# One-hot matrices and gated rows of a table building laid out token by token instead of eight tokens interleaved

## The chip, the cores and the metric

The kernel runs on one core of one Trainium2 chip. The metric is the device time of one launch in microseconds, the median of three runs. The engines work in parallel, each through its own list of instructions in order: TensorE (PE; its weight loads are PEld) multiplies matrices, VectorE (DVE) and ScalarE (ACT) work element by element, GpSimd (POOL) does some element work and issues the row gathers, SyncE (SP) issues the plain transfers.

## The reference

Two layers of a transformer over 512 latent tokens and 256 context tokens, 1024 wide. Each layer mixes tokens (three kinds of heads, one output projection) and then retrieves experts. The change touches the second part alone: each token has 8 heads, each head selects 16 of 16384 experts by a product key (two lists of 128 sub-keys, so an expert is a pair of numbers i and j below 128) and weighs them by a softmax.

```python
def peer(h, wq, subkeys, u, v):
    """sum_heads sum_topk g_e * gelu(u_e . h) * v_e."""
    ...
    s_top, i_top = lax.top_k(s, PEER_TOPK)
    cand = (s_top[:, :, 0, :, None] + s_top[:, :, 1, None, :]).reshape(...)
    ...
    best, pos = lax.top_k(cand, PEER_TOPK)
    expert = jnp.take_along_axis(cand_idx, pos, axis=-1)
    gate = jax.nn.softmax(best, axis=-1)
    ...
        a = jax.nn.gelu(jnp.einsum('cd,chkd->chk', hc, u[ec]), approximate=False)
        w = (gc * a).astype(v.dtype)
        return jnp.einsum('chk,chkd->cd', w, v[ec])
```

## The kernel before

Tokens stand in tiles of 128; the first layer has six (four latent, two context), the second four. After mixing and output projection, `peer` runs in stages.

A u-pass (`upass`, two halves of 64 columns of experts) multiplies the whole first expert matrix with three of the tiles and keeps the gelu of it, two tiles' worth in a table in SBUF, the third spilled to DRAM. These three tiles are called dense. The remaining tiles (three in the first layer, one in the second) are handled by gathers: `gather` fetches 128 expert rows a token, one DMA_INDIRECT for each of the 128 choices (L920, on GpSimd), and VectorE multiplies them with the token (L926). Gathers are generators, moved on at fixed rates between the other work.

Then a v-pass (`vpass`) for each pair of tiles multiplies a table over all experts (the summed gate of each expert, times the gelu) with the second expert matrix: 128 steps of 12 matmuls of 512 columns (L1060) in two halves. Each step loads a 128x1024 block, copies it to f16 on ScalarE (L1043) and takes the rest on GpSimd (L1047) or VectorE (L1045).

The table is built by `Scatter`. For a token the 128 choices stand along partitions; one-hot rows of i (128 wide) and of j (64 wide, the half of the table in work), the latter multiplied with the gate, are multiplied by TensorE and give the token's 128x64 table. The gate stands as two f16 parts whose sum is the f32 value, so a token takes two matmuls on the same one-hot weights (L1172 on the high part, L1173 on the low part). Eight tokens make one step: `oi` (L1167, 1024 elements a partition), `oj` (L1168, 512), `oh` and `ol` (L1169, L1170, 512 each) on VectorE, 16 matmuls into one PSUM tile `pw`, and then the evacuation into the table: VectorE multiplies it in (L1178, for the first pair), or ScalarE copies it (L1180, L1182) with VectorE taking the rest (L1183) for gathered tiles. All buffers but `oj` (one) are double. In `oi`, `oj`, `oh` and `ol` the eight tokens are the innermost dimension: element (k, x) belongs to choice number k and token x, and a matmul takes every eighth element.

`prep` (L1131 to L1145) brings a tile's choices and gates from tokens along partitions to choices along partitions through TensorE: `sT` holds i, j, the gate's high and its low part.

Where the steps stand is set by the generators in `vpass` and `upass`: after every second large step of a v-pass one step of the coming half's table is put into all engines' lists (`next(ahead, None)`), and in the second half of a u-pass from the twelfth step on by a rate (`SC0`). A half of a table is 32 steps: two tiles of 16. Ten such halves are built, five pairs of tiles in two halves each. The vector tables `st16` and `io16` are used by `pick`, which turns the top-16 lists into expert numbers.

Of the kernel before, what the change touches and what calls it, by code (L numbers as in the profile page):

```python
# [9 lines left out]
F16 = mybir.dt.float16  # L10
# [3 lines left out]
AF = mybir.ActivationFunctionType  # L14
OP = mybir.AluOpType
# [13 lines left out]
TB = 8  # L29
# [20 lines left out]
class Hybrid:  # L50
# [20 lines left out]
    # ---------------------------------------------------------------- constants  # L71
    def consts(self):
# [11 lines left out]
        self.iox = c.tile([128, 128, TB], F16, name="iox")  # L84
        nc.vector.tensor_copy(self.iox, io[:, :, None].to_broadcast([128, 128, TB]))
        self.io16 = c.tile([128, 16, 8], F16, name="io16")
        nc.vector.tensor_copy(self.io16, io[:, :16, None].to_broadcast([128, 16, 8]))
        self.st16 = c.tile([128, 2, 16, 8], F16, name="st16")
        prev = 0
        for a, s in enumerate((0, 16, 24, 29, 33, 36, 38, 40, 42, 43, 44, 45, 46, 47, 48, 49)):  # L90
            nc.vector.memset(self.st16[:, 0, a], float(s))
            nc.vector.memset(self.st16[:, 1, a], float(s - prev))
            prev = s
# [20 lines left out]
    def tick(self, gens, rate):  # L114
        """Moves the generators on by rate on the average."""
        self.due = getattr(self, "due", {})
        k = id(gens)
        self.due[k] = self.due.get(k, 0.0) + rate
        n = int(self.due[k])
        self.due[k] -= n  # L120
        self.step(gens, n)
# [57 lines left out]
    # ---------------------------------------------------------------- modulation  # L179
# [33 lines left out]
    def vectors(self, l, last, pool, ps):  # L213
        """The factors that vary along a row, written out as rows."""
        nc = self.nc
# [19 lines left out]
    # ---------------------------------------------------------------- layer  # L235
# [37 lines left out]
    # ---------------------------------------------------------------- mixers  # L273
# [203 lines left out]
    # ---------------------------------------------------------------- attention  # L477
# [171 lines left out]
    def strips(self, l, h, pool):  # L649
        """Decay by distance: forwards over positive, backwards over negative distances, both at zero."""  # L650
# [28 lines left out]
    # ---------------------------------------------------------------- output projection, second norm  # L679
# [80 lines left out]
    # ---------------------------------------------------------------- product-key routing  # L760
# [72 lines left out]

    def pick(self, l, t, sv, si, pool):
# [65 lines left out]
    # ---------------------------------------------------------------- gathered first expert matrix  # L900
# [35 lines left out]
    # ---------------------------------------------------------------- experts  # L936
# [4 lines left out]
    def peer(self, es, l, last, h2s):  # L941
# [10 lines left out]
        with ExitStack() as e:  # L952
            rp = self.pool(rk, "rk", 2)
            rt = self.pool(e, "rt", 2, side="right")
# [135 lines left out]
class Scatter:  # L1090
    """Sums the gates of a pair of tiles into a table over all experts; over given values the sums are multiplied in."""
# [7 lines left out]
    def col(self, half, jj, n=1):  # L1099
        """The table's columns jj.. of a half."""  # L1100
# [7 lines left out]
    def at(self, half, jj):  # L1108
        """The stationary operands of expert column jj: a pair of parts for each token tile."""
# [21 lines left out]
    def prep(self, t):  # L1131
# [10 lines left out]
        sT = o.sp.tile([128, 4, 128], F16, name="sT", bufs=2)  # L1142
        nc.scalar.activation(sT[:, 0:3], p[:, :384].rearrange("p (a b) -> p a b", b=128), AF.Copy)
        nc.vector.tensor_tensor(sT[:, 3], p[:, 256:384], sT[:, 2], op=OP.subtract)
        self.sT[t] = sT  # L1145

    def step(self, half):
# [6 lines left out]
        for s in sorted(range(2), key=lambda s: not self.dense[s]):  # L1154
# [3 lines left out]
            sT = self.sT[t]  # L1158
            for tb in range(0, 128, 8):
                pp = o.pw.tile([128, 8, 64], F32, name="pw")  # L1160
                for t0 in range(tb, tb + 8, TB):
                    oi = o.sp.tile([128, 128, TB], F16, name="oi")
                    oj = o.sp.tile([128, 64, TB], F16, name="oj", bufs=1)
# [92 lines left out]
```

## Time and profile before

| | us |
|---|---|
| median of three runs | 5032.78 (5029.45 to 5037.81) |
| the profiled execution, first to last instruction | 5040.9 |
| TensorE matmul busy | 4516.0 (90%) |
| TensorE weight load busy | 2857.2 (57%) |
| VectorE busy | 3624.2 (72%) |
| ScalarE busy | 2209.1 (44%) |
| GpSimd busy | 2221.1 (44%) |

A busy time is the union of an engine's recorded instructions. Matmuls overlap in the pipeline and their ends are modelled, so the pace of a burst is read from the starts of its instructions in the timeline. A row of the costliest groups gives line, engine, operation, tiles, shape and count, then busy us, mean ns, and the idle time before them with what ended it. A busy time of VectorE holds the time in which an instruction has been started and stands still.

### The profile page before, as it was taken

The numbers are of one execution on the slowest core, as the hardware profiler recorded it, in microseconds if no ns is written. First come the engines' busy times: TensorE is split into PE (matmuls) and PEld (weight loads), VectorE is DVE, ScalarE is ACT, GpSimd is POOL, SyncE is SP. The second block draws the span as 40 slices with busy tenths as digits, with TensorE's granted clock in tenths as the row PEclk, the third lists the DMA queues.
The fourth block names the chain that finished last, engine by engine and source line by source line (L and its number), as shares of the span: only waits on it lengthen the run. The fifth ranks groups of instructions, "written<-read, shape, count | busy, mean of one in ns | idle before, by whom it ended". The sixth has DMA issues, their size and how long they took to land. (4 is left out here: it accounts for less than half of the span.)

```text
span 5040.9 us, 79837 instructions
## 1 busy us (share of the span) xinstructions
PE 4516.0 (90%) x30416; PEld 2857.2 (57%) x30416; DVE 3624.2 (72%) x7163; ACT 2209.1 (44%) x3694; POOL 2221.1 (44%) x1493
## 2 busy tenths in 40 slices
PE   4987888978999988998899999788878999998998
PEld 3664566745665554554555467455545766655553
DVE  7777549897889999988798245745775777667543
ACT  5556344343433343433334466644444443343443
POOL 4224133457566665555233422422456544443333
PEclk9996999989999998999899999799999999998999
DMA  5421446668777767877578632144657764445555
GB/s 180 150 65 35 156 134 208 194 196 282 249 255 251 247 245 256 290 256 277 188 235 270 202 122 66 39 145 134 208 183 251 249 222 149 143 151 166 168 188 176
DMA packets 379873, 955.15 MB, mean 189 GB/s; under 512 B 43632, under 2 KB 158800, under 8 KB 379488
## 3 DMA queue, kind: packets, MB, share of 16 engines
q1 hardware_dynamic: 296000, 675.74, 41.6%
q0 software_dynamic: 73888, 268.53, 15.0%
q10 hardware_dynamic: 9600, 5.77, 0.4%
q8 instruction: 238, 3.90, 0.3%
q14 instruction: 147, 1.20, 0.1%
HBM read 920.49 MB, written 29.41 MB: 188 GB/s over the span
## 5 line engine op out<-in xcount | busy, mean ns | idle before, releaser
L1047 POOL TENSOR_TENSOR hl<-s,hl 128x1024 f16<-128x1024 f32 x384 | 861.8, 2244 | 1077.0 <-ACT hl L1043 1075.1
L1060 PE MATMUL acc<-hl,gst 128*128 128x512 f16 x3456 | 835.4, 391 | 17.6 <-DVE gst L149 9.0
L926 DVE SCALAR_TENSOR_TENSOR r<-r,hp 128x1024 f32<-128x1024 f32 x512 | 619.4, 1213 | 284.0 <-DMA r<-peer_u,ix 283.1
L1043 ACT ACTIVATE hl<-s 128x1024 f16<-128x1024 f32 x480 | 505.2, 1057 | 697.7 <-PE acc L1060 313.5
L1060 PEld LDWEIGHTS <-gst 128*128 128x128 f16 x4608 | 463.9, 101 | 565.6 <-issue 58.5
L920 POOL DMA_INDIRECT r<-peer_u,ix x512 | 547.2, 1069 | 391.5 <-DVE r L926 193.1
L1172 PE MATMUL pw<-oh,oi 128*128 128x64 f16 x2560 | 640.1, 300 | 72.0 <-DVE oh L1169 70.7
L1173 PE MATMUL pw<-ol,oi 128*128 128x64 f16 x2560 | 639.9, 301 | 13.7 <-DVE ol L1170 13.5
L1060 PE MATMUL acc<-hl,P 128*128 128x512 f16 x2304 | 558.5, 389 | 5.2 <-POOL hl L1047 3.1
L1060 PEld LDWEIGHTS <-P 128*128 128x128 f16 x3072 | 307.8, 100 | 354.1 <-issue 27.7
L1172 PEld LDWEIGHTS <-oi 128*128 128x128 f16 x2560 | 372.5, 146 | 133.9 <-DVE oh L1169 74.0
L174 PE MATMUL pw<-h2Uh,hl 128*128 128x384 f16 x1024 | 352.4, 344 | 56.4 <-ACT gst L1017 56.2
L1169 DVE TENSOR_TENSOR oh<-oj,sT 128x512 f16<-128x512 f16 x320 | 257.8, 806 | 201.8 <-PE pw L1172 197.5
L161 POOL TENSOR_TENSOR hl<-s,hl 128x1024 f16<-128x1024 f32 x136 | 299.0, 2200 | 227.0 <-ACT hl L160 173.3
L1173 PEld LDWEIGHTS <-oi 128*128 128x128 f16 x2560 | 373.4, 146 | 18.5 <-issue 1.5
L176 PE MATMUL pw<-h2Uh,hl 128*128 128x384 f16 x1024 | 351.8, 344 | 25.1 <-DVE hl L151 18.9
L176 PE MATMUL pa<-h2Uh,hl 128*128 128x384 f16 x1024 | 341.8, 334 | 34.7 <-POOL hl L161 34.6
L175 PE MATMUL pw<-h2Ul,hl 128*128 128x384 f16 x1024 | 351.7, 343 | 0.0
L174 PE MATMUL pa<-h2Uh,hl 128*128 128x384 f16 x1024 | 342.6, 335 | 1.5 <-ACT hl L160 1.5
L175 PE MATMUL pa<-h2Ul,hl 128*128 128x384 f16 x1024 | 341.1, 333 | 0.0
L176 PEld LDWEIGHTS <-hl 128*128 128x128 f16 x2048 | 207.0, 101 | 214.3 <-POOL hl L161 50.2
L1045 DVE TENSOR_TENSOR h2Ul<-h2Uh,h2Ul 128x1024 f16<-128x1024 f32 x160 | 233.6, 1460 | 130.3 <-ACT h2Ul L1043 130.3
(297 smaller groups left out, 9801.1 us busy)
## 6 DMA issues: line engine op xcount, KB each, us to landing
s<-peer_v SPq DMA_DIRECT2D x480, 512.0 KB
s<-ut SPq DMA_DIRECT2D x256, 512.0 KB
h2Uh<-peer_v SPq DMA_DIRECT2D x160, 512.0 KB
wq<-peer_wq SPq DMA_DIRECT2D x128, 256.0 KB
wst<-w_in SPq DMA_DIRECT2D x96, 256.0 KB
r<-w_ada SPq DMA_DIRECT2D x48, 512.0 KB
h2T<-w_ada SPq DMA_DIRECT2D x32, 512.0 KB
spill<-gst SPq DMA_DIRECT2D x64, 256.0 KB
```

The lines of the kernel that those rows point to most:

```text
L161: self.lo_ins = nc.gpsimd.tensor_tensor(lo, w, hi, op=OP.subtract)
L174: nc.tensor.matmul(out, ah, bh, start=start, stop=False)
L175: nc.tensor.matmul(out, ah, bl, start=False, stop=False)
L176: nc.tensor.matmul(out, al, bh, start=False, stop=stop)
L920: self.queue_behind(nc.gpsimd.indirect_dma_start(out=r, out_offset=None, in_=self.i["peer_u"], in_offset=bass.IndirectOffsetOnAxis(ap=ix[: ...
L926: nc.vector.scalar_tensor_tensor(r, r, 1.0, hp, op0=OP.mult, op1=OP.mult, accum_out=a[:, k - AHEAD:k - AHEAD + 1])
L1043: nc.scalar.activation(vh[:, 0], v, AF.Copy)
L1047: self.lo_ins = nc.gpsimd.tensor_tensor(vh[:, 1], v, vh[:, 0], op=OP.subtract)
L1060: nc.tensor.matmul(acc[s][hf], w, vh[:, x, hf * 512:hf * 512 + 512], start=j == 0 and i == 0, stop=j == 127 and i == 2)
L1169: nc.vector.tensor_tensor(oh, oj, col[2].to_broadcast([128, 64, TB]), op=OP.mult)
L1172: nc.tensor.matmul(pp[:, t0 - tb + x], oi[:, :, x], oh[:, :, x], start=True, stop=False)
L1173: nc.tensor.matmul(pp[:, t0 - tb + x], oi[:, :, x], ol[:, :, x], start=False, stop=True)
```

## The change

- `oi`, `oj` and the gated rows are laid out with the token outside and the expert number inside, so a matmul reads 128 or 64 neighbouring elements.
- `oh` and `ol` become one tile `og` of two parts, made by one instruction of 1024 elements.
- In `sT` the i and j of a choice stand twice, side by side; the two gate parts move to a tile `gT`, in blocks of eight tokens, each value twice. The VectorE instructions then work on pairs of neighbouring experts: of the slots they read the same pair again for each pair of experts.
- `iox`, the numbers 0 to 127, no longer stands eight times; `io16` and `st16` are built in `pick_tables`, once a layer, in a pool of the routing, with the memsets on GpSimd instead of VectorE.

```diff
-        self.iox = c.tile([128, 128, TB], F16, name="iox")
-        nc.vector.tensor_copy(self.iox, io[:, :, None].to_broadcast([128, 128, TB]))
-        self.io16 = c.tile([128, 16, 8], F16, name="io16")
-        nc.vector.tensor_copy(self.io16, io[:, :16, None].to_broadcast([128, 16, 8]))
-        self.st16 = c.tile([128, 2, 16, 8], F16, name="st16")
...
-            nc.vector.memset(self.st16[:, 0, a], float(s))
-            nc.vector.memset(self.st16[:, 1, a], float(s - prev))
+        self.iox = c.tile([128, 128], F16, name="iox")
+        nc.vector.tensor_copy(self.iox, io)
...
+    def pick_tables(self, pool):
+        nc = self.nc
+        self.io16 = pool.tile([128, 16, 8], F16, name="io16", bufs=1)
+        nc.vector.tensor_copy(self.io16, self.iox[:, :16, None].to_broadcast([128, 16, 8]))
+        self.st16 = pool.tile([128, 2, 16, 8], F16, name="st16", bufs=1)
+        prev = 0
+        for a, s in enumerate((0, 16, 24, 29, 33, 36, 38, 40, 42, 43, 44, 45, 46, 47, 48, 49)):
+            nc.gpsimd.memset(self.st16[:, 0, a], float(s))
+            nc.gpsimd.memset(self.st16[:, 1, a], float(s - prev))
+            prev = s
...
@@ peer
             rp = self.pool(rk, "rk", 2)
+            self.pick_tables(rp)
...
@@ Scatter.prep
-        sT = o.sp.tile([128, 4, 128], F16, name="sT", bufs=2)
-        nc.scalar.activation(sT[:, 0:3], p[:, :384].rearrange("p (a b) -> p a b", b=128), AF.Copy)
-        nc.vector.tensor_tensor(sT[:, 3], p[:, 256:384], sT[:, 2], op=OP.subtract)
-        self.sT[t] = sT
+        sT = o.sp.tile([128, 2, 128, 2], F16, name="sT", bufs=2)
+        nc.scalar.activation(sT, p[:, :256].rearrange("p (a b) -> p a b", b=128)[:, :, :, None].to_broadcast([128, 2, 128, 2]),
+                             AF.Copy)
+        gT = o.sp.tile([128, 128 // TB, 2, TB, 2], F16, name="gT", bufs=2)
+        g = p[:, 256:384].rearrange("p (n t) -> p n t", t=TB)[:, :, :, None].to_broadcast([128, 128 // TB, TB, 2])
+        nc.scalar.activation(gT[:, :, 0], g, AF.Copy)
+        nc.vector.tensor_tensor(gT[:, :, 1], g, gT[:, :, 0], op=OP.subtract)
+        self.sT[t] = sT, gT
@@ Scatter.step
-                    oi = o.sp.tile([128, 128, TB], F16, name="oi")
-                    oj = o.sp.tile([128, 64, TB], F16, name="oj", bufs=1)
-                    oh = o.sp.tile([128, 64, TB], F16, name="oh")
-                    ol = o.sp.tile([128, 64, TB], F16, name="ol")
-                    col = [sT[:, q, None, t0:t0 + TB] for q in range(4)]
-                    nc.vector.tensor_tensor(oi, o.iox, col[0].to_broadcast([128, 128, TB]), op=OP.is_equal)
-                    nc.vector.tensor_tensor(oj, ioj, col[1].to_broadcast([128, 64, TB]), op=OP.is_equal)
-                    nc.vector.tensor_tensor(oh, oj, col[2].to_broadcast([128, 64, TB]), op=OP.mult)
-                    nc.vector.tensor_tensor(ol, oj, col[3].to_broadcast([128, 64, TB]), op=OP.mult)
+                    oi = o.sp.tile([128, TB, 128], F16, name="oi")
+                    oj = o.sp.tile([128, TB, 64], F16, name="oj", bufs=1)
+                    og = o.sp.tile([128, 2, TB, 64], F16, name="og")
+                    for out, io, q, w2 in ((oi, o.iox, 0, 64), (oj, ioj, 1, 32)):
+                        nc.vector.tensor_tensor(out.rearrange("p t (i x) -> p t i x", x=2),
+                                                io.rearrange("p (i x) -> p i x", x=2)[:, None].to_broadcast([128, TB, w2, 2]),
+                                                sT[:, q, t0:t0 + TB, None].to_broadcast([128, TB, w2, 2]), op=OP.is_equal)
+                    g = gT[:, t0 // TB].rearrange("p z t x -> p (z t) x")
+                    nc.vector.tensor_tensor(og.rearrange("p z t (j x) -> p (z t) j x", x=2),
+                                            oj.rearrange("p t j -> p (t j)")[:, None].to_broadcast([128, 2, TB * 64])
+                                            .rearrange("p z (t j x) -> p z t j x", j=32, x=2),
+                                            g[:, :, None].to_broadcast([128, 2 * TB, 32, 2]), op=OP.mult)
                     for x in range(TB):
-                        nc.tensor.matmul(pp[:, t0 - tb + x], oi[:, :, x], oh[:, :, x], start=True, stop=False)
-                        nc.tensor.matmul(pp[:, t0 - tb + x], oi[:, :, x], ol[:, :, x], start=False, stop=True)
+                        nc.tensor.matmul(pp[:, t0 - tb + x], oi[:, x], og[:, 0, x], start=True, stop=False)
+                        nc.tensor.matmul(pp[:, t0 - tb + x], oi[:, x], og[:, 1, x], start=False, stop=True)
```

## Rows read from the trace of the kernel before

**Rows 1.** Busy us by stretch: length, engines (instructions), granted clock, DMA share, GB/s.
```profile
1098.00:1464.00 366.00, 327.14 (x2041) 215.88 (x2039) 302.13 (x502) 147.63 (x248) 221.22 (x157) 0.95 0.77 258
1469.00:1710.00 241.00, 233.94 (x1253) 137.11 (x1254) 236.76 (x330) 84.03 (x96) 167.70 (x98) 0.97 0.70 244
1716.00:1977.00 261.00, 238.57 (x1269) 138.97 (x1270) 246.34 (x325) 100.32 (x128) 159.41 (x99) 0.95 0.70 241
1990.00:2229.00 239.00, 232.39 (x1236) 135.04 (x1235) 214.47 (x342) 94.03 (x156) 133.76 (x92) 0.96 0.82 283
2230.00:2505.00 275.00, 244.81 (x1275) 140.40 (x1274) 216.16 (x362) 96.76 (x129) 120.48 (x78) 0.91 0.67 230
2517.00:2744.00 227.00, 224.62 (x1231) 133.22 (x1231) 219.04 (x331) 83.27 (x126) 79.57 (x34) 0.99 0.77 258
2746.00:2912.00 166.00, 166.00 (x772) 75.43 (x771) 45.71 (x51) 67.90 (x72) 64.93 (x32) 1.00 0.65 204
3806.00:4138.00 332.00, 316.07 (x2041) 213.28 (x2041) 231.86 (x347) 144.91 (x244) 190.99 (x131) 0.97 0.70 246
4143.00:4370.00 227.00, 226.83 (x1254) 135.83 (x1255) 159.08 (x231) 84.46 (x97) 105.58 (x48) 0.99 0.46 149
4373.00:4613.00 240.00, 232.25 (x1267) 137.74 (x1266) 160.19 (x234) 99.04 (x125) 99.65 (x45) 0.98 0.48 154
4631.00:4856.00 225.00, 225.00 (x1221) 132.08 (x1220) 120.30 (x237) 98.49 (x153) 77.38 (x33) 0.97 0.54 173
```

**Rows 2.** Waits in the first, fourth, eighth, ninth stretch: us, times, longest.
```profile
DVE r L926 <- DMA r<-peer_u,ix: 55.6, 38, 3.9
...
DVE r L926 <- DMA r<-peer_u,ix: 23.7, 13, 4.8
...
DVE r L926 <- DMA r<-peer_u,ix: 83.2, 48, 6.3
...
DVE oh L1169 <- PE pw L1172: 54.8, 29, 3.1
```

**Rows 3.** The page's costliest groups: the small matmul on the high part.
```profile
L1172 PE MATMUL pw<-oh,oi 128*128 128x64 f16 x2560 | 640.1, 300 | 72.0 <-DVE oh L1169 70.7
```

**Rows 4.** Timeline of one burst: start us, duration us, engine, line, operation.
```profile
1961.12 0.30 PE L1172 MATMUL pw<-oh,oi 128*128 128x64 f16 x1
...
1962.03 0.68 DVE L1167 TENSOR_TENSOR oi<-iox,sT 128x1024 f16<-128x1024 f16 x1
...
1962.63 0.41 DVE L1168 TENSOR_TENSOR oj<-iox,sT 128x512 f16<-128x512 f16 x1
...
1962.71 0.30 PE L1173 MATMUL pw<-ol,oi 128*128 128x64 f16 x1
...
1962.96 0.68 DVE L1183 TENSOR_TENSOR P<-pw,P 128x512 f16<-128x512 f32 x1
```

**Rows 5.** Timeline of TensorE in the attention, first and last of fifteen matmuls.
```profile
237.08 0.19 PE L174 MATMUL o<-nav,ph 128*128 128x64 f16 x1
...
237.49 0.19 PE L176 MATMUL o<-nav,pl 128*128 128x64 f16 x1
```

**Rows 6.** Two of the four lines: ns min/median/max, first and last start.
```profile
L1167 DVE TENSOR_TENSOR oi<-iox,sT x320: 672/682/3290, 1176.9 to 4843.5; 128x1024 f16<-128x1024 f16 x160
...
L1169 DVE TENSOR_TENSOR oh<-oj,sT x320: 406/425/3906, 1183.3 to 4843.1; 128x512 f16<-128x512 f16 x160
```

**Rows 7.** VectorE's groups by shape: one repeated word, and the unpacked rate.
```profile
L926 DVE SCALAR_TENSOR_TENSOR r<-r,hp 128x1024 f32<-128x1024 f32 x512 | 619.4, 1213 | 284.0 <-DMA r<-peer_u,ix 283.1
...
L847 DVE TENSOR_TENSOR cand<-sv 128x128 f32<-128x128 f32 x10 | 2.8, 280 | 0.0
```

**Rows 8.** Timeline: a VectorE instruction beside one of GpSimd.
```profile
1177.80 3.27 DVE L1167 TENSOR_TENSOR oi<-iox,sT 128x1024 f16<-128x1024 f16 x1
1178.38 2.13 POOL L161 TENSOR_TENSOR hl<-s,hl 128x1024 f16<-128x1024 f32 x1
```

**Rows 9.** Timeline of the start: a memset on GpSimd.
```profile
0.25 0.10 POOL L1248 MEMSET const-float32-0.0<- 128x1 f32 x1 [0.25 <-issue]
```

More of the change, by code (lines that the diff above doesn't have):

```diff
@@ L83, in consts @@
         nc.vector.tensor_scalar(self.idh, dl, 0.0, None, op0=OP.is_equal)
-        self.iox = c.tile([128, 128, TB], F16, name="iox")
-        nc.vector.tensor_copy(self.iox, io[:, :, None].to_broadcast([128, 128, TB]))
-        self.io16 = c.tile([128, 16, 8], F16, name="io16")
-        nc.vector.tensor_copy(self.io16, io[:, :16, None].to_broadcast([128, 16, 8]))
-        self.st16 = c.tile([128, 2, 16, 8], F16, name="st16")
-        prev = 0
-        for a, s in enumerate((0, 16, 24, 29, 33, 36, 38, 40, 42, 43, 44, 45, 46, 47, 48, 49)):
-            nc.vector.memset(self.st16[:, 0, a], float(s))
-            nc.vector.memset(self.st16[:, 1, a], float(s - prev))
-            prev = s
+        self.iox = c.tile([128, 128], F16, name="iox")
+        nc.vector.tensor_copy(self.iox, io)
         self.mhalf = c.tile([128, 8], F32, name="mhalf")
@@ L1157, in step @@
                 self.prep(t)
-            sT = self.sT[t]
+            sT, gT = self.sT[t]
             for tb in range(0, 128, 8):
```

## Prediction

> **What bounds the kernel now.** I read the totals of each stretch first, then the costliest groups, then single bursts in the timeline, and last who waits for whom. The change touches the building of the tables: ten stretches, two in the u-passes and eight in the v-passes, each with 512 small matmuls (32 steps of 16). The reader should see three kinds of stretch in [rows 1]. I name them A to J in order of time, and leave the one without table building out of the naming.
>
> In H, I and J (227, 240 and 225 us, second layer) TensorE is busy 97 to 100% and VectorE 53 to 70%: TensorE sets the end. In B, C, D and F VectorE is busy 237 of 241, 246 of 261, 214 of 239 and 219 of 227 us, and what D lacks is a wait for gathered rows of 23.7 us [rows 2]: there VectorE is as full as TensorE. A, E and G lie between: in A VectorE is busy 302 of 366 us and waits 55.6 us for gathers, in G it is busy 232 of 332 and waits 83.2 us [rows 2], while TensorE is busy 316 of G's 332. In H VectorE waits 54.8 us for TensorE to free the one-hot buffers [rows 2], so it has room there.
>
> How much the small matmuls take: the half of a v-pass without them takes 166.0 us for 768 large ones, all of it TensorE [rows 1]; the halves with them take 225 to 275. There are 2560 of L1172, and as many of L1173 on the other part [rows 3]. Their recorded 300 ns are mostly pipeline; the pace is read from starts. In one burst the first row here starts at 1961.12 and the 13th after it at 1962.71 [rows 4]: 1.59 us / 13 = 122 ns a matmul, with its weight load. 512 of them are 62.6 us of a stretch, and 166 + 62.6 = 229 is what H and J take.
>
> **The change, part by part.** *Matmul operands.* Before, the 128 weights and the 64 moving columns of a token lie 8 elements apart; after, side by side. The trace has the same matmul with packed operands in the attention: 128x64 f16 with a 128x128 f16 load each, alternating weights, starts 237.08 to 237.49 in 14 steps [rows 5], 29 ns each. So 122 - 29 = 93 ns go, 512 x 93 = 47.6 us per stretch, 476 us over ten if TensorE were the bound in all. A half with table building would be 166 + 15 = 181 us of TensorE. Bounds: nothing saved where another engine ends the stretch, 47.6 where TensorE does.
>
> The Trainium skill's "TensorE: Matmul & The Clock Gate", section on the back-to-back issue gap, gives about 81 ns for a sustained pair of load and 128-column matmul. By that the saving would be 41 ns a matmul and some 21 us a stretch (an estimate). The packed row above disagrees for this chip, and the sum goes by the row.
>
> *VectorE instructions.* Before, a block of 8 tokens takes four: one of 1024 elements (median 682 ns) and three of 512 (L1169: 425; L1168 and L1170 repeat it) [rows 6]. After, three: 1024, 512, and one of 1024 for both gated rows. In the pipeline a 1024 occupies 1962.63 - 1962.03 = 0.60 us and a 512 0.33 [rows 4], so a block goes from 0.60 + 3 x 0.33 = 1.59 to 1.53: 0.06 us, or 0.16 if medians are added up. 32 blocks: 2 to 5 us a stretch, if the new patterns keep the rate. They read the slots in pairs: two equal f16, one 4-byte word, again and again. The nearest row is the candidate sum L847, 128 f32 of which one input repeats a 4-byte word 16 times, 280 ns [rows 7], no more than such a size costs elsewhere in this kernel. That is one word a step without a penalty, but not with packed 16-bit pairs. The other end is the unpacked rate: 1024 elements 1213 ns (L926) [rows 7], 512 0.68 us (L1183) [rows 4]. Then a block takes 1.21 + 0.68 + 1.21 = 3.10 in place of 1.96 us: 1.14 us more, 36 us a stretch. I take the packed rate, because the word repeated at full rate is the nearer row; both ends stay for the range.
>
> *Waits on GpSimd.* The longest L1169 lasts 3906 ns and the longest L1167 3290 [rows 6]; one L1167 of 3.27 us starts at 1177.80 and ends 0.56 us after a GpSimd tensor operation that ran from 1178.38 to 1180.51 [rows 8]. A VectorE operation with two inputs in SBUF stands still until GpSimd's is over. GpSimd's work stays, so I expect the stall to move to the instruction that comes next, and take 0; one of four such instructions goes, so up to a quarter of the stall could go with it.
>
> *The rest.* The small tables are built in each layer: 32 memsets on GpSimd, 0.10 us each by the nearest row [rows 9], 3 us a layer at the end of the mixers, queued ahead of the first splits of routing weights; if the buffer's former owner is late, those wait with it. Bound 0 to 5 us a layer; I take 0. The start loses as many memsets and 7/8 of one copy on VectorE: about 1 us, taken as 0. Each of ten tile preparations gains one ACT operation and wider ones, bounded by three operations of 0.68 us, 2 us each beside matmuls: 0 to 20, taken as 0. DMAs and queues are not touched.
>
> *The sum by stretch.* H, I, J: TensorE falls to 181 us plus what it idles now; VectorE's 159, 160 and 120 us fit below. 44 + 44 + 43 = 131. G: VectorE's 232 fit, its 83 us of waiting for gathers must shrink to let TensorE's gain through: I take 40 of 47.6. A: VectorE's 302 busy plus at least some 40 of its 55.6 us of waits leave 24. E: TensorE idles in it already; about half, 22. B, C, D, F: only VectorE's own gain and a little coupling: 5 + 9 + 6 + 6 = 26. Together 131 + 40 + 24 + 22 + 26 = 243. The profiled execution spans 5040.9 us; 5041 - 243 = 4798. Its span stands 8 us above the median of the timed runs, so 4790. What is late next: VectorE in the first layer, large matmuls in the second.
>
> **Rivals.** *All lands.* VectorE's fullness in the first layer is a matter of order and of GpSimd's stalls, and yields when TensorE does. For it: TensorE is 97 to 99% busy in B, D and F too. Against: VectorE has no idle time there to give. If the other 476 - 243 came half, 4670; all, 4560.
>
> *Pairs lose the packed rate* (the slower side). Place: the three VectorE instructions of each block; price 36 us a stretch. B, C, D and F, full already, grow by 36, 28, 36 and 36 (C gives up some TensorE idle time), A by 25, E by 14, G by 0 (gather waits absorb it against the TensorE gain). H: 159 + 36 + 7 of other waits = 202, so -25; I -16; J 120 + 36 < 181, still -43. Sum +91, 5124. It decides from about 0.8 us more a block: between -243 at no price and +91 at 1.14 us the sum crosses zero there, and the first layer loses what the second gains. For it: no row has a two-element row of 16-bit data. Against: L847's repeated word.
> The Trainium skill's "Vector Engine (DVE) Microarchitecture Reference", section on measured stream behaviour, says that a port streams at full rate only in runs of at least two adjacent 4-byte words; the slots now come as runs of one. By its table (1.73 against 1.05 ns a step) a block would gain about 0.7 us, an estimate just short of the point named; L847 shows no such loss for a repeated word, so it does not raise the chance much.
>
> *Transfers or gathers close in.* The DMA engines are 0.77 and 0.82 busy in A and D [rows 1]; if gathers land later as the stretches shorten, A, E and G keep their times and only 131 + 26 are left: 4876.
>
> **How the numbers follow.** Chances: forecast 0.72, all lands (more than half of the rest) 0.08, transfers 0.10, pairs at the lower rate 0.10 (in two thirds of that slower, else near no change or slightly faster). The forecast's own range is 4700 to 4870: below, a quarter of the GpSimd stall and some coupling in B to F; above, H to J at three quarters and A, E and G at half. The range to hold 8 in 10 takes in half of "all lands" and the transfers: 4670 to 4900. About 0.2% (10 us) is what can be told from no change. Faster 0.91, same 0.02, slower 0.07.
>
> **What would show it.** Small matmuls starting about 29 ns apart; H, I and J near 181 to 196 us; B, D and F within 10 us of before, with VectorE still full and TensorE's waits for the gated rows grown; three VectorE instructions a block at 682, 425 and 682 ns medians. The prediction is wrong if the gated-row instruction takes over 1 us at its median, if the matmul pace stays above 60 ns, or if B, D and F shrink by 30 us and more.

## The result and the profile after

The changed kernel takes 4869.93 us (median of four runs, 4854.72 to 4873.35), the kernel before on the same chip 5031.11: a ratio of 0.9668 [0.9654, 0.9681]. That is 161 us saved where 243 were forecast. The profiled executions span 5040.9 and 4871.5 us, a difference of 169.4.

The ten stretches with table building and the one without, with the columns of [rows 1]:

```profile
1114.00:1467.00 353.00, 290.99 (x2041) 171.37 (x2039) 279.95 (x464) 146.40 (x252) 223.91 (x156) 0.93 0.78 264
1478.00:1714.00 236.00, 192.50 (x1248) 90.25 (x1246) 234.10 (x296) 83.12 (x95) 166.26 (x98) 0.96 0.68 246
1721.00:1970.00 249.00, 201.17 (x1267) 94.45 (x1265) 239.47 (x285) 97.61 (x129) 161.06 (x99) 0.89 0.72 249
1988.00:2223.00 235.00, 194.00 (x1230) 89.80 (x1230) 207.44 (x305) 90.59 (x154) 133.95 (x91) 0.95 0.83 284
2224.00:2474.00 250.00, 198.41 (x1270) 92.92 (x1269) 227.93 (x327) 97.25 (x134) 126.82 (x78) 0.93 0.72 253
2491.00:2701.00 210.00, 186.95 (x1220) 88.34 (x1220) 193.15 (x293) 80.43 (x122) 76.85 (x33) 0.99 0.79 269
2701.00:2873.00 172.00, 168.33 (x787) 75.98 (x786) 48.18 (x56) 70.29 (x75) 67.20 (x34) 0.99 0.64 203
3760.00:4067.00 307.00, 275.32 (x2042) 166.00 (x2041) 223.47 (x310) 142.61 (x247) 197.66 (x132) 0.97 0.76 263
4074.00:4271.00 197.00, 185.70 (x1251) 89.65 (x1252) 191.75 (x201) 83.51 (x95) 114.56 (x48) 0.98 0.53 170
4273.00:4478.00 205.00, 187.49 (x1282) 91.83 (x1283) 188.53 (x199) 96.91 (x129) 108.18 (x45) 0.97 0.57 178
4494.00:4681.00 187.00, 181.01 (x1211) 88.31 (x1209) 140.76 (x203) 90.76 (x150) 86.28 (x33) 0.99 0.64 206
```

Against [rows 1] A to F give 13, 5, 12, 4, 25 and 17 us, G to J 25, 30, 35 and 38: 204 in all. The reader should see two things. TensorE's busy time falls in every one of the ten by 36 to 46 us, not far from the 47.6 forecast. And in H and I, where TensorE alone set the end, VectorE's busy time has *grown*, from 159.08 and 160.19 to 191.75 and 188.53, although it has fewer instructions (201 for 231): it is now the fullest engine there.

The small matmuls and what VectorE does for them. The timeline of one burst in H (start us, duration us), with the neighbours of VectorE and GpSimd:

```profile
4101.36 5.01 POOL L1052 TENSOR_TENSOR hl<-s,hl 128x1024 f16<-128x1024 f32 x2 [3.52 <-ACT hl L1048]
4101.77 2.62 DVE L1180 TENSOR_TENSOR og<-oj,gT 128x1024 f16<-128x1024 f16 x1
...
4102.57 0.19 PE L1185 MATMUL pw<-og,oi 128*128 128x64 f16 x1
...
4103.01 0.19 PE L1186 MATMUL pw<-og,oi 128*128 128x64 f16 x1
```

Sixteen matmuls start within 4103.01 - 4102.57 = 0.44 us: 29 ns apart, as in [rows 5]. The gated rows `og` meanwhile take 2.62 us beside a GpSimd operation. Undisturbed they take 0.68, as the medians of the three lines show (ns min/median/max, first and last start):

```profile
L1176 DVE TENSOR_TENSOR oi<-iox,sT x320: 674/682/4935, 1194.7 to 4674.8; 128x1024 f16<-128x1024 f16 x160
...
L1176 DVE TENSOR_TENSOR oj<-iox,sT x320: 404/417/5076, 1195.3 to 4673.8; 128x512 f16<-128x512 f16 x160
L1180 DVE TENSOR_TENSOR og<-oj,gT x320: 671/680/5083, 1199.1 to 4676.8; 128x1024 f16<-128x1024 f16 x160
```

In H alone, the groups of VectorE's instructions (busy us, mean ns):

```profile
L141 DVE TENSOR_TENSOR gst<-P,gst 128x512 f16<-128x512 f32 x32 | 48.5, 1518 | 0.2 <-ACT gst L139 0.2
L1180 DVE TENSOR_TENSOR og<-oj,gT 128x1024 f16<-128x1024 f16 x31 | 42.5, 1371 | 0.0
L1176 DVE TENSOR_TENSOR oi<-iox,sT 128x1024 f16<-128x1024 f16 x31 | 40.2, 1297 | 0.0
...
L1191 DVE TENSOR_TENSOR P<-pw,P 128x256 f32<-128x256 f32 x61 | 22.8, 413 | 3.2 <-PE pw L1186 3.2
```

The means of the first three are twice what the instructions need. What this costs TensorE stands in its waits in H and, second line, in I (us, times, longest):

```profile
PE pw L1185 <- DVE og L1180: 11.3, 7, 2.0
...
PE acc L1065 <- DVE h2Ul L1050: 11.7, 4, 5.0
```

The 11.3 us for the gated rows are all that TensorE idles in H (197.0 - 185.7), and `h2Ul` in I is VectorE's output too: TensorE waits for VectorE there, not for GpSimd's own results. The last group of the list, L1191, which has one input in PSUM, is not delayed at all. Nor are the 512 products of gathered rows, whose other input `hp` lies in PSUM, anywhere in the kernel:

```profile
L930 DVE SCALAR_TENSOR_TENSOR r<-r,hp x512: 1192/1210/1223, 810.3 to 4061.0; 128x1024 f32<-128x1024 f32 x171
```

Take for each kind of VectorE instruction the time that its fastest tenth stays within, and add up over a stretch what each instruction took beyond that. The sum is called the *stall* here: 49, 45 and 6 us in H, I and J before, 85, 78 and 29 after.

Two smaller losses lie outside the ten stretches. The first matmul of the first u-pass starts 14 us later; in the groups of the line of that matmul (first and last start) the kernel before has

```profile
L174 PE MATMUL pw<-h2Uh,hl x1024: 322/326/528, 606.6 to 3805.1; 128*128 128x384 f16 x171
```

and the changed one

```profile
L166 PE MATMUL pw<-h2Uh,hl x1024: 322/326/528, 620.7 to 3759.9; 128*128 128x384 f16 x171
```

And the two halves of v-passes without table building are 172 us instead of 166: the 41st matmul starts 14.3 and 14.9 us after the first instead of 8.65, because TensorE now arrives before the last columns of the table have been copied. The waits of TensorE at the start of the second of them make up most of this (us, times, longest):

```profile
PE acc L1065 <- ACT P L1195: 4.0, 1, 4.0
PE acc L1065 <- DVE P L1196: 0.7, 1, 0.7
```

So 204 - 14 - 12 = 178; three seams between stretches grew by 5 us each and others gave a little back, which leaves the 169 of the spans.

### The profile page after: what moved, and what is told of

It is laid out like the page before. It is cut to its first block, busy times and chain, and to the rows that moved or that the text cites. A ratio compares the mean times of both kernels' runs of the same rounds, so it can differ in the third digit from the quotient of the medians.

```text
span 4871.5 us, 79464 instructions
## 1 busy us (share of the span) xinstructions
PE 4102.9 (84%) x30416; PEld 2392.5 (49%) x30416; DVE 3665.2 (75%) x6812; ACT 2188.7 (45%) x3704; POOL 2269.5 (47%) x1557
## 5 line engine op out<-in xcount | busy, mean ns | idle before, releaser
L1052 POOL TENSOR_TENSOR hl<-s,hl 128x1024 f16<-128x1024 f32 x384 | 880.1, 2296 | 873.8 <-ACT hl L1048 856.6
L924 POOL DMA_INDIRECT r<-peer_u,ix x512 | 572.1, 1117 | 428.7 <-DVE r L930 219.3
L1065 PEld LDWEIGHTS <-gst 128*128 128x128 f16 x4608 | 452.5, 100 | 607.4 <-issue 116.0
L1065 PEld LDWEIGHTS <-P 128*128 128x128 f16 x3072 | 296.3, 99 | 428.7 <-issue 95.0
L153 POOL TENSOR_TENSOR hl<-s,hl 128x1024 f16<-128x1024 f32 x136 | 299.0, 2200 | 170.1 <-ACT hl L152 85.1
L1185 PE MATMUL pw<-og,oi 128*128 128x64 f16 x2560 | 203.8, 197 | 205.7 <-DVE og L1180 199.1
L1050 DVE TENSOR_TENSOR h2Ul<-h2Uh,h2Ul 128x1024 f16<-128x1024 f32 x160 | 259.4, 1621 | 123.7 <-ACT h2Ul L1048 123.7
L1176 DVE TENSOR_TENSOR oi<-iox,sT 128x1024 f16<-128x1024 f16 x320 | 321.9, 1006 | 27.5 <-PE pw L1186 26.3
L1065 PE MATMUL acc<-h2Ul,gst 128*128 128x512 f16 x1152 | 289.6, 395 | 53.9 <-DVE h2Ul L1050 53.9
L151 ACT ACTIVATE s<-s 128x1024 f32<-128x1024 f32 x136 | 143.7, 1057 | 417.7 <-DMA s<-ut 392.7
L1180 DVE TENSOR_TENSOR og<-oj,gT 128x1024 f16<-128x1024 f16 x320 | 322.5, 1008 | 0.6
```

The lines of the kernel that those rows point to most:

```text
L153: self.lo_ins = nc.gpsimd.tensor_tensor(lo, w, hi, op=OP.subtract)
L924: self.queue_behind(nc.gpsimd.indirect_dma_start(out=r, out_offset=None, in_=self.i["peer_u"], in_offset=bass.IndirectOffsetOnAxis(ap=ix[: ...
L1050: nc.vector.tensor_tensor(vh[:, 1], v, vh[:, 0], op=OP.subtract)
L1052: self.lo_ins = nc.gpsimd.tensor_tensor(vh[:, 1], v, vh[:, 0], op=OP.subtract)
L1065: nc.tensor.matmul(acc[s][hf], w, vh[:, x, hf * 512:hf * 512 + 512], start=j == 0 and i == 0, stop=j == 127 and i == 2)
L1176: nc.vector.tensor_tensor(out.rearrange("p t (i x) -> p t i x", x=2), io.rearrange("p (i x) -> p i x", x=2)[:, None].to_broadcast([128, TB ...
```

## The experiments

The theory: the packed matmuls do what was forecast, but GpSimd's splits of the value blocks (the subtraction that makes a block's low part) and VectorE's operations with both inputs in SBUF take turns (theory A), and once TensorE is fast this sets H and I. Twelve kernels, in the order in which they are argued.

**Which operand made the 122 ns.** Two kernels read one operand of the small matmuls at the old spacing.

```diff
-  matmul(pp[...], oi[:, x], og[:, 0, x], ...)
+  matmul(pp[...], oi[:, x], og[:, 0].rearrange("p t j -> p (t j)")[:, x::TB], ...)        # cols_strided
+  matmul(pp[...], oi.rearrange("p t i -> p (t i)")[:, x::TB], og[:, 0, x], ...)           # weights_strided
```

cols_strided: 

> The changed kernel, but the small matmuls read their 64 moving columns at the old spacing (every eighth element of the packed rows; the table's contents lose their meaning, the instructions are the same in number and size). The weights stay side by side. Theory W, the strided weight load made the old 122 ns: the small matmuls still start 28 to 45 ns apart, H, I and J stay near 197, 205 and 187 us, total 4855 to 4890. Rival C, the strided moving columns made it: the pace goes back to some 122 ns, H, I and J go back to 226, 240 and 225, total 4990 to 5060. Rival B, each has a share: pace 60 to 95 ns, and because VectorE is as full as TensorE in H and I, a part of it hidden: total 4890 to 4990.

weights_strided: 

> The changed kernel, but the small matmuls load their 128 weights at the old spacing (every eighth element of the packed one-hot rows; contents lose their meaning, instructions the same in number and size). The moving columns stay side by side. Theory W: the pace goes back to some 122 ns, H, I and J to 226, 240 and 225 us, total 4990 to 5060. Rival C: pace stays at 28 to 45 ns, total 4855 to 4890. Rival B: pace 60 to 95 ns, total 4890 to 4990.

Measured: 5006.26 and 4894.66 us, one run each. The timelines of a burst, first the strided columns, then the strided weights:

```profile
4603.06 0.30 PE L1186 MATMUL pw<-og,oi 128*128 128x64 f16 x1
...
4604.81 0.29 PE L1185 MATMUL pw<-og,oi 128*128 128x64 f16 x1
```

```profile
4515.01 0.23 PE L1186 MATMUL pw<-og,oi 128*128 128x64 f16 x1
...
4516.03 0.22 PE L1185 MATMUL pw<-og,oi 128*128 128x64 f16 x1
```

1.75 us for 15 steps is 117 ns; 1.02 us for 17 steps is 60 ns. Theory W, the weights, was wrong; the columns make nearly all of it (rival C). Rival C missed in the second kernel, though: at 60 ns and 4894.66 us it lies where rival B put it, so the weights alone would still cost 31 ns. Both strided take 122, neither 29: the costs don't add up, the longer one covers most of the other. H, I and J go back to 222, 239 and 222 us with strided columns.

**Taking GpSimd away.** In the v-passes ScalarE copies the block a second time in place of GpSimd's subtraction, of which 16 of 1024 columns are left; so this kernel leaves out the low part of those blocks.

```diff
-  self.lo_ins = nc.gpsimd.tensor_tensor(vh[:, 1], v, vh[:, 0], op=OP.subtract)
+  nc.scalar.activation(vh[:, 1], v, AF.Copy)
+  self.lo_ins = nc.gpsimd.tensor_tensor(vh[:, 1, :16], v[:, :16], vh[:, 0, :16], op=OP.subtract)
```

> The changed kernel; in the v-passes GpSimd's low-part split of 1024 columns is cut to 16 columns, and ScalarE copies the block in place of the rest, so the low part of those blocks is not computed. Theory A (VectorE stands behind GpSimd's tensor operations): VectorE's stalls in H, I, B and C (85, 78, 75, 77 us) fall below 15 us each, H and I go to TensorE's 183 to 188, B from 236 to under 205, C from 250 to under 220, total about 4870 - 120 = 4750 or less. Theory B (the order of VectorE's list, or gathers, hold B and C): H and I within 10 us of now, B above 225, total above 4830.

Measured: 4650.92 us, one run. Stalls are at most 2 us in every stretch of the v-passes, and H, I and J become alike, all of it TensorE (columns of [rows 1]):

```profile
3904.00:4084.00 180.00, 179.66 (x1247) 89.04 (x1248) 109.23 (x199) 128.78 (x144) 12.38 (x48) 1.00 0.61 194
4087.00:4268.00 181.00, 180.80 (x1280) 89.85 (x1279) 114.52 (x201) 138.57 (x173) 20.56 (x45) 1.00 0.64 204
4282.00:4464.00 182.00, 180.61 (x1209) 88.36 (x1207) 115.15 (x208) 125.40 (x186) 7.15 (x33) 0.99 0.68 216
```

That is the 181 us of the prediction's "TensorE falls to 181". B to F fall too, to 187, 201, 214, 226 and 186: their fullness was for a large part stalling.

**Moving work from GpSimd to VectorE.** If the two take turns, a split on VectorE (1.22 us) should be cheaper for VectorE itself than the same on GpSimd (2.14 us at the median). Where both tiles of a pair are dense (B, C, H and I), VectorE splits one of four blocks in the changed kernel; here two of four:

```diff
-VDVE = ((1, 3), (1, 3), (3,))
+VDVE = ((1, 3), (1, 3), (1, 3))
```

> The changed kernel; in the v-passes whose two tiles are dense (stretches B, C, H, I) half of the low-part splits go to VectorE instead of a quarter: 16 splits a stretch leave GpSimd (2.13 us each) for VectorE (1.22 us). Theory A, that H and I now end when the sum of GpSimd's tensor operations and VectorE's operations with two SBUF inputs is done (H: 102 + 86 = 188 of 197 us, I: 96 + 101 = 197 of 204): that sum falls by 16 x 0.91 = 15 us, H to about 185 and I to about 191, B and C by 5 to 15, total 4870 - 35 = 4835, range 4815 to 4850. Theory B, that VectorE's own instructions set the end and the stall behind GpSimd is idle time under another name: 19 us more work a stretch, H, I, B and C each 5 to 19 us longer, total 4890 to 4930.

Measured: 4811.82 us (4808.02 to 4813.17), ratio to the kernel before 0.9563 [0.9543, 0.9584]. More work on the fullest engine, and 58 us less than the change alone, where theory A expected 35 (the total lies 3 us below its range): VectorE's stall in H goes from 85 to 2 us and H from 197 to 183, B and C from 236 and 249 to 224 and 228. D gets 9 us longer.

**All of them, and three of four** (on top of start_and_split, further down).

```diff
-VDVE = ((1, 3), (1, 3), (1, 3))
+VDVE = ((0, 1, 2, 3), (0, 1, 2, 3), (0, 1, 2, 3))    # all_on_vector
+VDVE = ((0, 1, 3), (0, 1, 3), (0, 1, 3))             # three_on_vector
```

all_on_vector: 

> On top of the last combination (4804): GpSimd makes none of the low parts of the value blocks in the v-passes, VectorE makes all. Theory A (the two engines take turns at data in SBUF): each move takes away 2.13 us of GpSimd and adds 1.15 us to VectorE, so the turns shrink and the stalls go to about 2 us a stretch, as in the run without the GpSimd part; the bound is then VectorE's own work, which comes to some 222, 218, 222, 228 and 208 us in B to F and 162, 160 and 147 in H to J, and TensorE's 182. So D 248 to 225, E 250 to 232, H, I and J 182, the two halves without table building 171 to 166, B and C within 13 us of before, F within 5: total 4725, range 4700 to 4770. Rival V (VectorE is the scarce engine in the first layer, so 37 us more per stretch cost there about what they cost): B, C, D and E at 245 to 270, total 4820 to 4900.

three_on_vector: 

> The same with three of four blocks on VectorE and one on GpSimd (1 in 4). Theory A: half of the way between 4804 and the run with all on VectorE, or better, since both engines have room: about 4765, range 4735 to 4800; stalls 10 to 25 us a stretch. Rival V: 4810 to 4850.

Measured: 4732.57 us (4729.26 to 4737.19), ratio 0.9399 [0.9384, 0.9415], and 4782.86 us (4768.78 to 4787.48), 0.9494 [0.9472, 0.9516]; both lie in theory A's ranges. With all on VectorE B, D, E, F, H, I and J are:

```profile
1458.00:1672.00 214.00, 191.06 (x1248) 88.89 (x1248) 211.71 (x343) 85.47 (x96) 54.72 (x48) 0.99 0.81 274
...
1912.00:2138.00 226.00, 194.61 (x1259) 87.06 (x1257) 212.13 (x352) 96.87 (x156) 57.27 (x55) 0.99 0.85 297
2143.00:2408.00 265.00, 205.13 (x1276) 90.97 (x1274) 226.91 (x368) 96.22 (x131) 49.75 (x46) 0.94 0.73 243
2421.00:2607.00 186.00, 183.56 (x1232) 89.14 (x1231) 184.15 (x294) 83.57 (x122) 0.00 (x0) 0.98 0.78 260
...
3982.00:4163.00 181.00, 181.00 (x1247) 89.35 (x1246) 164.74 (x250) 83.44 (x95) 0.00 (x0) 0.99 0.59 192
4166.00:4347.00 181.00, 180.44 (x1268) 89.46 (x1266) 161.38 (x236) 96.18 (x127) 0.00 (x0) 1.00 0.62 195
4365.00:4547.00 182.00, 181.27 (x1233) 89.45 (x1233) 154.59 (x246) 94.78 (x153) 0.00 (x0) 0.99 0.69 219
```

In H VectorE makes 49 splits more than in the changed kernel, 60 us of work, and yet is busy 165 us where it was 192. Its groups in H:

```profile
L1054 DVE TENSOR_TENSOR hl<-s,hl 128x1024 f16<-128x1024 f32 x49 | 59.9, 1222 | 2.4 <-ACT hl L1052 2.4
...
L151 DVE TENSOR_TENSOR gst<-P,gst 128x512 f16<-128x512 f32 x32 | 21.8, 685 | 0.0
L1184 DVE TENSOR_TENSOR og<-oj,gT 128x1024 f16<-128x1024 f16 x31 | 21.3, 686 | 0.0
```

`og` is at 686 ns for 1371, `gst` at 685 for 1518. One part of what was expected failed: E became longer (250 to 265), not shorter, as rival V has it for one stretch of four. VectorE's stall there is 3 us, and it is busy 227 of 265; why E grew is not settled. And of the two halves without table building only the second falls to 166 us; the first takes 173.

**The same edit without the change.** This is the control: were the turns there before, and what did they cost?

```diff
 (kernel before)
-VDVE = ((1, 3), (1, 3), (3,))
+VDVE = ((0, 1, 2, 3), (0, 1, 2, 3), (0, 1, 2, 3))
```

> The kernel before, with only the splitting edit: VectorE makes all low parts of the value blocks in the v-passes, GpSimd none. The same edit on the changed kernel (with the start's order) gave 4855 to 4733, 123 us. Theory A (the turns of VectorE and GpSimd were there before the change, but in H, I and J lay in TensorE's shadow, and only the packed matmuls brought them to the path): stalls go to about 2 us a stretch here too, yet H and J stay at TensorE's 226, I loses 5 to 14, and B, D and F end near 229 to 240 instead of 240, 239 and 227, C and E give up some 15 to 30 together: total 4975 to 5015. Rival E (the split on GpSimd cost the same before as after): 123 us here too, 4900 to 4925. Rival O (it cost nothing before): 5020 to 5045.

Measured: 5027.3 us (5021.93 to 5033.59), ratio 0.9986 [0.9977, 0.9996]. The edit that gives 123 us on the changed kernel (4855.28, with the start as before, to 4732.57) gives 6 on the kernel before, under the 10 us that the prediction named as what can be told from no change. So theory A's size of 18 to 58 us failed, and the total lies in the range of rival O, that the split cost nothing before. Its rows show more than the total: C (261 to 237) and I (240 to 226) gain as theory A has it, but B, D and E lose 7, 4 and 9. The stall is 3 us or less in every stretch with table building of the v-passes here too, H's 49 among them, and H stays as it was (227 to 226). Why B, D and E grew is not settled. G, H, I and J of this run:

```profile
3806.00:4139.00 333.00, 317.31 (x2047) 213.52 (x2045) 236.20 (x349) 145.83 (x247) 188.27 (x130) 0.98 0.71 245
4142.00:4368.00 226.00, 226.00 (x1252) 135.49 (x1251) 167.80 (x281) 84.13 (x96) 0.00 (x0) 0.99 0.47 151
4372.00:4598.00 226.00, 225.85 (x1265) 136.69 (x1264) 167.11 (x274) 98.82 (x125) 0.00 (x0) 1.00 0.50 159
4614.00:4836.00 222.00, 221.79 (x1222) 131.41 (x1221) 159.21 (x276) 99.13 (x155) 0.00 (x0) 0.99 0.57 178
```

With GpSimd's subtractions out of the v-passes in both, the change takes H, I and J from 226, 226 and 222 to 181, 181 and 182: 45 + 45 + 40 = 130 us, where the prediction's three terms were 131. And the step from one kernel to the other is worth 5027 - 4733 = 294 us in all instead of 161, though all_on_vector also has another start (below).

**The start.** Two kernels ask where the 14 us ahead of the first u-pass come from. The first is the kernel before with the moved small tables alone:

```diff
 (kernel before, consts)
-        self.io16 = c.tile([128, 16, 8], F16, name="io16")
...
 (peer)
+            self.pick_tables(rp)
```

> The kernel before with one part of the change alone: the two small tables are built in pick_tables each layer, the rest stays interleaved. Leading theory: the 14 us that the changed kernel comes late to its first u-pass matmul (621 against 607 us) are the price of this part; the instruction lists of the mixers stand in another order since it moved, and that order is the same in this kernel and in the changed one. It expects the first u-pass at 621 us, plus or minus 4, and 5031 + 14 = 5045 us, plus or minus 6. Rival, that the late start is chance of one execution: first u-pass at 607 and 5031 plus or minus 6.

Measured: 5044.06 us (5034.45 to 5057.66) beside 5034.14, ratio 1.0024 [1.0008, 1.0039], and its first u-pass starts as late as that of the changed kernel:

```profile
L166 PE MATMUL pw<-h2Uh,hl x1024: 322/326/528, 621.2 to 3816.9; 128*128 128x384 f16 x171
```

The second is the changed kernel with the memsets back on VectorE at the start, and two copies of the old sizes there whose results nobody reads:

```diff
 (changed kernel, consts)
+        iod = tmp.tile([128, 128, TB], F16, name="iod")
+        nc.vector.tensor_copy(iod, io[:, :, None].to_broadcast([128, 128, TB]))
...
+        self.st16 = c.tile([128, 2, 16, 8], F16, name="st16")
...
```

> The changed kernel with VectorE's work at the start as it was: the 32 memsets of the one table are back there, and two copies of the old size write tiles that nobody reads. The list order of the mixers is then a third one, neither that of the kernel before nor that of the changed one. If the order of the lists sets the 14 us, the first u-pass starts somewhere from 600 to 625 us and the total moves with it (4850 to 4875); if the 14 us come from the table part's own instructions, it starts at 607 and the total is 4856.

Measured: 4855.28 us (4841.90 to 4867.01), ratio 0.9659 [0.9633, 0.9686]; the first u-pass starts at

```profile
L176 PE MATMUL pw<-h2Uh,hl x1024: 322/326/528, 608.6 to 3729.1; 128*128 128x384 f16 x171
```

More work at the start, and 12 us earlier. The totals of this kernel and of the changed one can't be told apart (their intervals overlap), so the 12 us are read from the first u-pass alone. The expectation's other reading, the table part's own instructions, names the same time (607 us), and this run by itself doesn't exclude it. The traces do: in the changed kernel the memsets run on GpSimd from 610.3 to 611.3 us, but its 800th matmul already starts at 177.0 us, against 164.1 in the kernel before and 167.5 here. Without the constants at the start the matmuls of the mixers run in another order, different from the 20th on and the same in tables_only as in the changed kernel. The seven kernels with that order start the first u-pass at 617.6 to 621.5 us, the seven others at 604.2 to 610.8, and the granted clock of the first 600 us doesn't sort them: 0.88 goes with 604.2 in before_all_on_vector, 0.91 with 619.8 in two_gated_rows. So the order is 12 to 14 us slower. Which wait in the mixers it is was not traced.

**Both gains together.**

```diff
 (start_as_before)
-VDVE = ((1, 3), (1, 3), (3,))
+VDVE = ((1, 3), (1, 3), (1, 3))
```

> Two edits that each gained by itself, together: the list order of the start (4855 against 4870 with the change alone) and more of the splitting of table rows taken from GpSimd to VectorE in the second part of the last pass (4812). If they are independent, as the explanations say (one sits ahead of the first u-pass, the other in the v-passes), 4812 - 14 = 4798, range 4785 to 4812. Rival: what the first saves ahead of the u-pass is given back later as waiting of TensorE, as 12 us were in the halves without table building: 4808 to 4820.

Measured: 4804.16 us (4795.03 to 4808.62), ratio 0.9550 [0.9531, 0.9569]. 8 us below split_on_vector instead of 14; the ranges of the two expectations overlap here, and this run doesn't tell them apart.

**The fusing undone.** The changed kernel with two instructions for the gated rows.

```diff
-                    nc.vector.tensor_tensor(og.rearrange("p z t (j x) -> p (z t) j x", x=2),
...
+                    for z in range(2):
+                        nc.vector.tensor_tensor(og[:, z].rearrange("p t (j x) -> p t j x", x=2),
...
```

> The changed kernel with the gated rows made by two VectorE instructions of 512 elements per block in place of one of 1024. Its list order in the mixers is that of the changed kernel. By medians a block has 682 + 417 + 2 x 417 in place of 682 + 417 + 680 ns: 0.15 us more, 0.06 by the burst, 32 blocks: 2 to 5 us a stretch, in the seven stretches B to F, H and I where VectorE is full 14 to 35 us at most. Theory A (stall behind GpSimd is bound to the total time of the GpSimd tensor operations, not to the number of VectorE instructions): total 4880 to 4900. Rival N (each instruction more is one more chance to stand still, so a quarter more stalling): stalls grow by some 60 us over the stretches, total 4920 to 4950. Rival 0 (nothing, the two hide): 4865 to 4875.

Measured: 4887.23 us (4882.07 to 4890.31), ratio 0.9718 [0.9700, 0.9736] beside 0.9668 of the change. Theory A: the stalls in B to F, H and I sum to 432 us beside 425, so one instruction more does not stall more; the 17 us fit its own time (2 to 5 us a stretch), though B alone grows by 12 and F by 8. It is the prediction's "up to a quarter of the stall could go" that falls here.

**One more place.** In all_on_vector GpSimd still takes the low parts in half of the u-passes.

```diff
 (all_on_vector)
-UPOOL = ((), (1, 2))
+UPOOL = ((), (1,))
```

> On top of all_on_vector (4733): in the second half of each u-pass, one of three blocks instead of two of three takes its low part from GpSimd (VectorE makes the other; its scaling on ScalarE goes with it). Theory A: some 13 blocks a pass move, the turns of the two engines in A and G (188 and 172 us with GpSimd) lose 13 us each, and TensorE, which waits for GpSimd's low parts there, gains: A 352 to 340 to 348, G 304 to 296 to 302, total 4710 to 4730. Rival G: A and G are held by the gathered rows (69.8 and 82.9 us of waits for them), VectorE has no room in A, nothing is gained: 4728 to 4745.

Measured: 4742.46 us (4725.93 to 4746.89), ratio 0.9408 [0.9382, 0.9434]: no gain. A and G are 353 and 309 us, GpSimd's busy time 21 to 24 us less:

```profile
1096.00:1449.00 353.00, 289.01 (x2040) 169.58 (x2039) 290.20 (x484) 134.42 (x239) 201.59 (x144) 0.93 0.78 266
3680.00:3989.00 309.00, 275.75 (x2052) 165.88 (x2051) 227.07 (x327) 129.94 (x233) 171.78 (x117) 0.97 0.75 261
```

Rival G fits: VectorE's stall falls from 48 to 40 us in A and from 37 to 27 in G, and neither gets shorter. all_on_vector stays the fastest version, 137 us below the changed kernel.

## Why the prediction was right in direction and short in size

The 4869.93 us stand at the edge of the forecast's own range, 4700 to 4870. Of the signs that the prediction named, the 29 ns and the three medians came, and none of its signs of being wrong did; H and I (197 and 205 us) lie above its 181 to 196, and F moved by 17 us, not within 10.

**Matmul operands: right.** 122 to 29 ns, 93 saved, TensorE at 181 us in a half. The Trainium skill's "TensorE: Matmul & The Clock Gate", section on the back-to-back issue gap, gives 81 ns for a sustained pair of load and 128-column matmul; the pairs here, of 64 columns, start 29 ns apart through a whole burst, so that figure is no floor for them.

**VectorE's instructions: right.** 682, 417 and 680 ns at the median, 682, 425 and 682 forecast. The rival of the lost packed rate, with its 1.21 us for the gated rows, is out. So is, for a single word that is read again and again, what the prediction weighed beside it from the Trainium skill's "Vector Engine (DVE) Microarchitecture Reference", section on measured stream behaviour (its estimate of 0.7 us is small: a block reads 256 + 512 + 512 words from the slots, and 1280 times 0.68 ns, by the same table, are 0.87).

**The failed step: "GpSimd's work stays, so I expect the stall to move to the instruction that comes next, and take 0".** The stall did not only move, it grew, in H by 36 us, in I by 33, in J by 23. Before, VectorE in H was idle 54.8 us behind TensorE [rows 2], and GpSimd's 102 us of subtractions (48 of 2.13) ran partly in that idle time. After, VectorE is hardly let off: it waits 3.2 us for TensorE. GpSimd's 102 us and VectorE's own 86 us of instructions with two inputs in SBUF (estimated without stalls and at the spacing of starts, 0.60 us for a recorded 0.68) take turns, 102 + 86 = 188 of H's 197 us; in I 96 + 101 = 197 of 205. So "VectorE's 159, 160 and 120 us fit below" was counted with the wrong sum: what must fit is GpSimd's time plus the share of VectorE's that takes turns with it. The prediction even had the row, 3.27 us of L1167 beside GpSimd [rows 8]. The two terms of H and I came out at 30 and 35 instead of 44 each, J's at 38 of 43; all_on_vector against its control shows 45, 45 and 40. (By the prediction's own rule, 181 us plus what TensorE idles now, I's term would have been 240 - 189 = 51, not 44.) The Trainium skill's "SBUF — State Buffer", section "Who interferes with whom", states that an instruction of VectorE with two SBUF inputs contends with a GpSimd instruction that reads SBUF, and that the order of issue decides which of the two is blocked. The rows above agree, also in that an input from PSUM (413 and 1210 ns) goes free. So does a count over the changed kernel: of the instructions for `oi`, `oj` and `og` that overlap a tensor operation of GpSimd, 152 of the 182 that started behind it took over 0.8 us, and 24 of the 98 that started ahead of it.

**G and A: too much by 15 and 11.** "its 83 us of waiting for gathers must shrink" did not happen: VectorE waits 84.2 us for gathers in G and 71.3 in A after, 83.2 and 55.6 before [rows 2]. G still gained 25 us; TensorE was the fuller engine there. With the turns out of the v-passes A and G are 351 and 304, hardly better than 353 and 307, so the shortfall is not the same cause. That the gathers hold them fits, but no run took the gathers away.

**B to F: 26 + 22 forecast, 63 measured.** F gave 17 for 6, with VectorE's stall there down from 49 to 29: the same turns, falling the other way. That stalls move from stretch to stretch by such amounts was no term at all.

**"The rest", taken as 0: 14 us.** The bound for the moved tables was 0 to 5 us a layer, worked out from the memsets. The memsets took 1 us; what cost was the order of other instructions, which no term counted. The 12 us at the start of the halves without building are also no term: a stretch that ends sooner hands its backlog to the next.

**The rivals.** "Transfers close in" gave 4876, 6 us from the measured time, but by another mechanism: it kept A, E and G and gave H, I and J in full; measured, these three lose 28 of 131, while A, E and G give 63. That it came near is chance. "All lands" was right on one point, that VectorE's fullness in the first layer was in part GpSimd's stalls; but it did not yield with TensorE, it yielded with GpSimd. Together: H to J 28 short, A and G 26, B to F 15 over, start 14, halves 12, seams 9: 74 of the spans' 243 - 169.

## What to carry to other kernels

When the bounding engine is sped up, do not compare the next engine's busy time with the new length: add to it what it must wait for in turn, here GpSimd's subtractions and VectorE's instructions with two inputs in SBUF, which take turns. A stall that lies in the shadow of another engine costs next to nothing (6 us of 5033 here) until the shadow goes (123 us), and then even work moved *onto* the fullest engine can shorten the kernel. Make the operands of small matmuls contiguous first of all on the moving side.

## What the runs showed of the hardware

- 64 f16 moving columns at a spacing of 16 bytes: 117 ns a matmul, 1.8 ns a column; 128 f16 weights at that spacing: 60 ns a matmul with its load; both: 122; neither: 29.
- VectorE's f16 instruction keeps its packed rate (1024 elements in 0.68 us) when one input is a single pair read again for 32 or 64 steps.
- GpSimd's row gathers don't delay VectorE, only its tensor operations do, about 2 us at a time: in the changed kernel 255 instructions for `oi`, `oj` and `og` overlap a gather and no other instruction of GpSimd, and the longest takes 0.74 us; of the 280 that overlap a tensor operation, 176 take over 0.8. In the timeline of A, `oi` inside a gather takes 0.68 us, and `oj` right behind it, at the next subtraction, 2.76 instead of 0.42:

```profile
1233.34 0.68 DVE L1176 TENSOR_TENSOR oi<-iox,sT 128x1024 f16<-128x1024 f16 x1
1233.94 2.76 DVE L1176 TENSOR_TENSOR oj<-iox,sT 128x512 f16<-128x512 f16 x1
...
1233.02 1.23 POOL L924 DMA_INDIRECT r<-peer_u,ix  x1 [0.16 <-issue]
1234.27 2.13 POOL L153 TENSOR_TENSOR hl<-s,hl 128x1024 f16<-128x1024 f32 x1
```
